# A SwiGLU block on one core: the down stage's first sums, a page's low part, and the second pair's stores and rebuilding steps rearranged

## Chip, cores and metric

The kernel runs on one core of a Trainium2 chip. The metric is the time of one execution on the device in microseconds (us), as the median of several runs. The engines are called TensorE (PE; its weight loads are PEld), VectorE (DVE), ScalarE (ACT), GpSimd (POOL) and SyncE (SP, which issues loads).

## What is computed

One transformer layer and a last norm, on x of 1024 tokens by 1024 channels, fp32. The change works in the last product pair of the layer, the SwiGLU:

```
mixed = jnp.concatenate([attn, pool], axis=-1)
x = x + jnp.einsum('bse,ed->bsd', mixed, w_out[layer])
h2 = rmsnorm(x, norm2_g[layer])
gate = jnp.einsum('bsd,df->bsf', h2, w_gate[layer])
up = jnp.einsum('bsd,df->bsf', h2, w_up[layer])
x = x + jnp.einsum('bsf,fd->bsd', jax.nn.silu(gate) * up, w_down[layer])
return rmsnorm(x, final_g)
```

D_FF is 2816. Ahead of it stand forgetting attention, a pooling mixer and the output projection, which the change does not touch.

## The kernel before

**Split products.** Each fp32 operand is split into a high part, which ACT copies out (line 120), and a low part, which DVE forms as operand minus high (line 121). A product is then three matmuls (`mm3`): high by high (L161), L162 and L163, each with one of the two low parts. A split operand is called a page; names end in `_h` and `_l`. A DVE instruction for a page of 128x1024 reads two operands from SBUF.

**Gate and up.** The 2816 columns are worked off in 11 pairs j = 0 to 10 of 2 x 128 columns. A pair is a Strassen scheme of seven products P1 to P7 between blocks of the turned activations (b11, b21, b22, t1 to t4) and a page of weights or of weight sums (`gu_page`; names `gu{j}_P1` and so on). POOL forms the weight sums s1 to s4 of the next pair from the raw loads r0 and r1 (L1091). From pair 2 on P3, and from pair 3 on P2 too, is itself done as seven quarter products Q1 to Q7 (banks `fineA`, `fineB`, `fineC`), each followed by an addition on DVE (L1289) from PSUM into an SBUF tile. A bank is used again by the next quarter, so TensorE waits for that addition. The pages of P3 come in two parts, a and b; their 128x256 sums (`fine_sums`, L1245) are on DVE but for part b of pair 10, which is on POOL. For b21 the quarter operands are rebuilt once, by a list of DVE steps (`fine_steps`, L1214, L1221; tiles `fine_b21..`, `fine2l_b21`, `b21l`) during pairs 1 and 2; the table `PACE` says how many steps are issued after each product.

**Order of work.** `todo` lists all (j, product). From pair 3 on the order is P1, P7, P2a, P6, P2b, P5, P3a, P4, P3b; in pairs 1 and 2 it is P1, P2, P6, P7, P5, P3a, P4, P3b. The page of an entry is issued two entries ahead (`next_page(*todo[i + 2])`), so page P1 of the next pair is issued at P4. A scheduler orders the instructions of each engine; `tc.issue_after(x)` keeps an instruction behind x. `mark` holds the last instruction of a kind: "page" (a low part), "hi" (a high part), "add" (a quarter's addition). The quarters Q5, Q6 and Q3 of P3 close a pair: their additions stand on DVE beside the low part of the next pair's P1.

**Features.** ACT, DVE and POOL turn the products into silu(gate) * up in the form that the down stage's own Strassen scheme wants: h11, h21, h22 (L1181, L1182) and f1 to f4 (L1190), which POOL forms. `spill` stores them to a scratch in DRAM (`hsdP1` to `hsdP7`, L1293), from ACT's queue, those of pair 10 from POOL's.

**Down stage.** The pairs are taken in four groups, (0, 1), (2, 3, 4), (5, 6, 7) and (8, 9, 10), each again with seven products in the order P1, P2, P6, P7, P5, P4, P3. Step i has a page of weights (tiles `d{i}_2` high, `d{i}_3` low) and one of features loaded back (`r_f{i}`; `d{i}_0` high, `d{i}_1` low), both made by `down_page(i)`. `down_sum` (L1379) forms the weight sums for P5, P6, P7 and P4 from the raw weights `r_wd0`, `r_wd1`; for the first group all four are on POOL, for the others on DVE. DVE adds the results to the residual (L1670). The first down page is made while pair 10 ends.

Of the kernel before, what the change touches and what calls it, by code (L numbers as in the profile page):

```python
# [30 lines left out]
NG = NF // 2  # L31
# [14 lines left out]
def tile_kernel(  # L46
# [952 lines left out]
    def gu_page(name, src, raw=None, cols=1024):  # L999
        n = count[0]  # L1000
        count[0] += 1
        hi, lo = page((("wh", "wl"), ("wh", "wl"), ("wr", "wr"))[n % 3], name)
        if cols < 1024:
            src = src.rearrange("p g e -> p (g e)")[:, 0:cols]
            mark["page"] = split(hi[:, 0:cols], lo[:, 0:cols], src)
            return hi, lo
        h2, l2 = (t.rearrange("p (g e) -> p g e", g=2) for t in (hi, lo))
        if raw:
            r = vpool.tile([P, 2, 1024], F32, tag=raw, bufs=1, name=f"r_{name}")[:, :, 0:512]
            for g in range(2):  # L1010
# [229 lines left out]
    def fine_sums(j, k, part, eng=nc.vector):  # L1240

        p0, p1, p2, p3 = (operands[j][k][:, n, h] for n in range(2) for h in QTR)
        later = ((p2, p3, p2, ALU.subtract), (p1, p1, p2, ALU.subtract), (p0, p0, p2, ALU.add))
        for out, in0, in1, op in ((p2, p0, p2, ALU.subtract),) if part == "a" else later:
            ins = eng.tensor_tensor(out=out, in0=in0, in1=in1, op=op)  # L1245
            mark["sum" if eng is nc.vector else "aside"] = ins
        summed.add((j, k, part))
# [50 lines left out]
    def after(j, k):  # L1298
# [12 lines left out]
        if k == "P2b":  # L1311
# [3 lines left out]
            nc.gpsimd.tensor_tensor(out=acc[1], in0=acc[1], in1=acc[0], op=ALU.mult)  # L1315
# [59 lines left out]
    def down_sum(b, k):  # L1375
        a0, a1 = dict(P5=("b12", "P1"), P6=("P3", "P5"), P7=("P3", "b12"), P4=("P2", "P6"))[k]
        t = blk_tile(SUMS[k], [P, len(GROUPS[b]), 512], F32, f"sum{k}_{b}")
        eng = nc.vector if b else nc.gpsimd
# [16 lines left out]
    def down_page(i):  # L1395
# [4 lines left out]
        lows = low, split(fh, fl, raw2.pop(i))  # L1400
# [20 lines left out]
    def next_page(j, k):  # L1421
        if (j, k) not in pages:
            if k[-1] in "ab":
                pages[j, k] = fine_page(j, k[:2], k[-1])
            else:
                pages[j, k] = gu_page(f"gu{j}_{k}", operands[j][k])
# [9 lines left out]
    PACE = {(1, "P1"): 1, (1, "P2"): 3, (1, "P6"): 3, (1, "P7"): 3, (2, "P1"): 2, (2, "P2"): 2, (2, "P6"): 1, (2, "P4"): 2, (2, "P3b"): 3}  # L1436
    waiting = []
    for i, (j, k) in enumerate(todo):
        shown = mark["page"]
        if i + 2 < len(todo) and (j < BOTH or k not in ("P1", "P2a")) and (j < BOTH - 1 or k != "P3a"):  # L1440
            with ExitStack() as order:
# [5 lines left out]
                if j >= BOTH and k in ("P7", "P6", "P2b", "P5"):  # L1447
                    if k == "P5":
                        fine_sums(j, "P3", "b", nc.vector if j < NG - 1 else nc.gpsimd)
# [4 lines left out]
                next_page(*todo[i + 2])  # L1454
# [6 lines left out]
        if j < BOTH:  # L1461
            while len(waiting) > 1:
                with tc.issue_after(mark["hi"].ins), tc.issue_after(mark["snap"].ins) if j == 2 else ExitStack():
# [42 lines left out]
        if j == NG - 1:  # L1506
# [20 lines left out]
        for _ in range(min(PACE.get((j, k), 2 if j < 2 else 0), len(finer))):  # L1527
            with tc.issue_after((shown if j == 2 and k != "P2" else mark["page"] if j else mark["h22", 0]).ins):
# [96 lines left out]
    for i, (b, k) in enumerate(steps2):  # L1625
# [3 lines left out]
        if b and k in ("P1", "P2", "P6") and (b, k) != (1, "P1"):  # L1629
# [85 lines left out]
```

## Time and profile before

| what | us |
|---|---|
| median of 3 runs | 1041.72 (1040.68 to 1042.95) |
| the profiled execution | 1040.65 |
| its span | 1038.9 |
| DVE busy | 776.1 (75%) |
| ACT busy | 471.6 (45%) |
| POOL busy | 405.5 (39%) |

The profile is that of one execution, and its instruction times are counted from the start of the span; 1.75 us of the execution lie outside it. In the timeline an engine's row gives start, duration, line, operation, and output <- input with partitions x elements. Numbers of tiles are left out there (`gu_P_l` is a low page of any pair); in the listings of the order below they stand, with a serial number behind. A bracket at the end of a row gives the idle time ahead of it and what released it. A DVE or POOL row starts when the instruction begins, also where it then stands still for another engine, so its duration can hold a wait. The rows of the windows give, for a stretch of time, each engine's busy time and count, the TensorE clock that was granted as a share of full speed, the share of time that the DMA engines were busy, and the GB/s.

### The profile page before, as it was taken

To read this page: it belongs to the slowest core of one execution; us is meant where nothing else is said; L and a number is where in the kernel's file an instruction comes from. 1 tells how busy PE (TensorE), PEld (TensorE's weight loads), DVE (VectorE), ACT (ScalarE), POOL (GpSimd) and SP (SyncE) were. 2 spreads that over 40 slices of the span, in tenths; PEclk is the share of its full clock that TensorE was granted. 3 is DMA by queue.
4 is the path that set the end of the run, shared out by engine and by line. 5 is a ranking of instruction groups with operands and counts; after the bars stand their busy time and mean duration, and the time that the engine had idled before them with its cause. 6 is when DMAs were issued, how large, how long until landed. Compare 5 with 4: busy or idle time off the path is not lost.

```text
span 1038.9 us, 15118 instructions
## 1 busy us (share of the span) xinstructions
PE 1022.6 (98%) x5428; PEld 878.7 (85%) x5428; DVE 776.1 (75%) x1219; ACT 471.6 (45%) x759; POOL 405.5 (39%) x322
## 2 busy tenths in 40 slices
PE   9999999999999999999999999999999899999997
PEld 8988888998888888888788888888888678888886
DVE  7465566776886488986977776876775899888887
ACT  7434355655665266442343443334334333333346
POOL 4350121213345042547547546555566900000045
PEclk9999999999999999999999999999999999999999
DMA  7214424233742142342223342332346764353424
GB/s 250 53 49 141 106 79 115 71 104 85 252 160 90 59 149 84 96 136 96 79 82 105 107 131 75 112 123 75 108 132 224 263 243 152 129 194 102 153 92 162
DMA packets 108795, 130.28 MB, mean 125 GB/s; under 512 B 8040, under 2 KB 71024, under 8 KB 108720
## 3 DMA queue, kind: packets, MB, share of 16 engines
q1 hardware_dynamic: 97216, 108.18, 33.3%
q10 hardware_dynamic: 10784, 19.16, 4.8%
q0 software_dynamic: 720, 1.97, 0.6%
q8 instruction: 43, 0.70, 0.3%
q14 instruction: 32, 0.26, 0.1%
HBM read 86.29 MB, written 33.03 MB: 115 GB/s over the span
## 4 chain that ended last, share of the span: by engine, by line
PE 95%; DVE 2%; issue 1%; DMA 1%; POOL 0%; ACT 0%; POOLq 0%; SPq 0%; DVEq 0%; ACTq 0%
PE gu_P L161 10%; PE gu_P L162 10%; PE gu_P L163 10%; PE d L162 6%; PE d L163 6%; PE d L161 6%; PE po L657 3%; PE tp L643 3%; PE o L161 3%; PE qk L162 3%; PE qk L163 3%; PE qk L161 3%; PE o L162 3%; PE o L163 3%; PE v L374 2%; PE z L618 2%
## 5 line engine op out<-in xcount | busy, mean ns | idle before, releaser
L162 PE MATMUL d<-d,d 128*128 128x512 f32 (+1 forms) x308 | 120.1, 391 | 4.7 <-DVE d L121 4.7
L163 PE MATMUL d<-d,d 128*128 128x512 f32 (+1 forms) x308 | 119.7, 390 | 0.0
L629 POOL TENSOR_SCALAR p<-p,rr 128x128 f32<-128x128 f32 (+3 forms) x64 | 48.5, 763 | 175.2 <-DVE rr L628 143.0
L161 PE MATMUL d<-d,d 128*128 128x512 f32 x308 | 108.3, 389 | 0.0
L120 ACT ACTIVATE d<-r_f 128x1536 fp32r<-128x1536 f32 (+1 forms) x28 | 38.8, 1384 | 119.0 <-PE d L162 114.3
L162 PEld LDWEIGHTS d<-d,d 128*128 128x128 f32 x308 | 58.3, 189 | 17.4 <-DVE d L121 5.3
L121 DVE TENSOR_TENSOR gu_P_l<-s,gu_P_h 128x1024 fp32r<-128x1024 f32 (+1 forms) x38 | 60.6, 1604 | 14.2 <-ACT gu_P_h L120 14.0
L1566 POOL TENSOR_SCALAR sse<-sse 128x1 f32<-128x1 f32 x7 | 3.5, 493 | 172.0 <-ACT junk L1562 172.0
L163 PEld LDWEIGHTS d<-d,d 128*128 128x128 f32 x308 | 58.3, 189 | 12.0
L161 PEld LDWEIGHTS d<-d,d 128*128 128x128 f32 x308 | 58.1, 189 | 12.0
L626 ACT ACTIVATE p<-p,mn 128x128 f32<-128x128 f32 (+3 forms) x64 | 49.3, 772 | 32.4 <-DVE mn L620 29.5
L121 DVE TENSOR_TENSOR gu_P_l<-r,gu_P_h 128x1024 fp32r<-128x1024 f32 x24 | 55.0, 2294 | 8.4 <-ACT gu_P_h L120 5.5
L121 DVE TENSOR_TENSOR d<-r_f,d 128x1536 fp32r<-128x1536 f32 (+1 forms) x28 | 54.7, 1954 | 7.0 <-ACT d L120 7.0
L648 DVE TENSOR_TENSOR tl<-tp,th 128x512 fp32r<-128x512 f32 (+1 forms) x80 | 49.4, 633 | 10.6 <-ACT th L647 9.6
L120 ACT ACTIVATE gu_P_h<-s 128x1024 fp32r<-128x1024 f32 (+1 forms) x38 | 36.4, 964 | 41.0 <-POOL f L1190 7.2
L1670 DVE TENSOR_TENSOR x2f_s<-d,x2f_s 128x512 f32<-128x512 f32 x64 | 42.6, 685 | 11.2 <-PE d L163 11.2
L163 PE MATMUL qk<-hTh,l_qk 128*128 128x512 f32 x128 | 50.7, 396 | 0.0
L161 PE MATMUL qk<-hTh,h_qk 128*128 128x512 f32 x128 | 50.6, 395 | 0.0
L162 PE MATMUL qk<-hTl,h_qk 128*128 128x512 f32 x128 | 50.4, 394 | 0.0
L647 ACT ACTIVATE th<-tp 128x512 fp32r<-128x512 f32 (+1 forms) x80 | 42.4, 550 | 14.9 <-PE tp L643 12.2
L1154 ACT ACTIVATE sn_sU<-gu_P 128x512 f32<-128x512 f32 x44 | 26.2, 595 | 45.6 <-PE gu_P L163 45.5
L620 DVE CUSTOM_DVE_ANT_0 p<-z,wmask 128x128 f32<-128x128 f32 (+3 forms) x64 | 33.7, 535 | 13.4 <-PE z L618 9.5
(1180 smaller groups left out, 3351.7 us busy)
## 6 DMA issues: line engine op xcount, KB each, us to landing
r_f<-hsdP SPq DMA_DIRECT2D x77, 256.0 KB
r<-in_w_gate_dram SPq DMA_DIRECT2D x44, 256.0 KB
r<-in_w_up_dram SPq DMA_DIRECT2D x44, 256.0 KB
r_wd<-in_w_down_dram SPq DMA_DIRECT2D x22, 512.0 KB
hsdP<-f ACTq DMA_DIRECT2D x40, 256.0 KB
s<-hi SPq DMA_DIRECT2D x64, 128.0 KB
hsdP<-h ACTq DMA_DIRECT2D x23, 256.0 KB
x<-in_x_dram SPq DMA_DIRECT2D x8, 512.0 KB
```

The lines of the kernel that those rows point to most:

```text
L120: mark["hi"] = nc.scalar.activation(out=hi, in_=src, func=AF.Copy)
L121: return eng.tensor_tensor(out=lo, in0=src, in1=f32(hi), op=ALU.subtract)
L161: nc.tensor.matmul(ps, lh, rh, start=start, stop=False, **kw)
L162: nc.tensor.matmul(ps, lh, rl, start=False, stop=False, **kw)
L163: mark["mm"] = nc.tensor.matmul(ps, ll, rh, start=False, stop=stop, **kw)
L620: nc.vector.tensor_tensor_reduce(out=pr[:, n0:n1], in0=z, in1=wmask[:, S - n + n0 : S - n + n1], scale=1.0, scalar=mn, op0=ALU.add, op1=AL ...
L626: nc.scalar.activation(out=pr[:, :n], in_=pr[:, :n], func=AF.Exp, scale=-1.0, bias=mn, accum_out=rs)
L629: nc.gpsimd.tensor_scalar(out=pr[:, :n], in0=pr[:, :n], scalar1=rr, scalar2=1.0, op0=ALU.mult, op1=ALU.mult)
L643: nc.tensor.transpose(tp[:, w : w + P], probs[h, 2 * sb + a][:, s * P : (s + 1) * P], ident)
L647: nc.scalar.activation(out=th[:, :w], in_=tp[:, :w], func=AF.Copy)
L648: nc.vector.tensor_tensor(out=tl[:, :w], in0=tp[:, :w], in1=f32(th[:, :w]), op=ALU.subtract)
L1670: added = nc.vector.tensor_tensor(out=row, in0=ps, in1=row, op=ALU.add)
```

## The change

Six parts:

1. `gu_page` takes `between`. For page P1 of pairs 3 to 10 the low part is made in two instructions of 128x512, and the second is kept behind the addition of the quarter issued last (the Q6 of P3).
2. The 128x256 sums for part b of P3 in pair 10 go from POOL to DVE.
3. The four weight sums of the first group are divided: P5 on DVE, behind page P5 of pair 10; P6 and P7 on POOL, behind the product h11 of pair 10; P4 on DVE, in the down stage at step P6.
4. `down_page(0)` is issued one entry later, at P4, and its feature low part d0_1 is kept behind a quarter's addition.
5. `PACE`: rebuilding steps of b21 that were issued at P4 and P3b of pair 2 are issued at P6 and P7.
6. The stores of pair 1's features, and of P1 and P4 of pair 2, are no longer issued entry by entry in pair 2, but at P7, P3a, P4 and P3b by the rule of the later pairs.

```diff
@@ -996,7 +996,7 @@
 
-    def gu_page(name, src, raw=None, cols=1024):
+    def gu_page(name, src, raw=None, cols=1024, between=None):
         n = count[0]
@@ -1013,6 +1013,13 @@
                 mark["page"] = split(h2[:, g, :], l2[:, g, :], src[g])
+        elif between is not None:
+            mark["hi"] = nc.scalar.activation(out=h2, in_=src, func=AF.Copy)
+            for g in range(2):
+                with tc.issue_after(between.ins) if g else ExitStack():
+                    mark["page"] = nc.vector.tensor_tensor(
+                        out=l2[:, g, :], in0=src[:, g, :], in1=f32(h2[:, g, :]), op=ALU.subtract
+                    )
         else:
@@ -1237,13 +1244,12 @@
 
-    def fine_sums(j, k, part, eng=nc.vector):
+    def fine_sums(j, k, part):
 
...
         for out, in0, in1, op in ((p2, p0, p2, ALU.subtract),) if part == "a" else later:
-            ins = eng.tensor_tensor(out=out, in0=in0, in1=in1, op=op)
-            mark["sum" if eng is nc.vector else "aside"] = ins
+            mark["sum"] = nc.vector.tensor_tensor(out=out, in0=in0, in1=in1, op=op)
         summed.add((j, k, part))
@@ -1312,7 +1318,7 @@
                 nc.scalar.activation(out=acc[0], in_=acc[0], func=AF.Silu)
-            nc.gpsimd.tensor_tensor(out=acc[1], in0=acc[1], in1=acc[0], op=ALU.mult)
+            mark["h11"] = nc.gpsimd.tensor_tensor(out=acc[1], in0=acc[1], in1=acc[0], op=ALU.mult)
             feats["h11"] = acc[1]
@@ -1372,10 +1378,9 @@
 
-    def down_sum(b, k):
+    def down_sum(b, k, eng=nc.vector):
         a0, a1 = dict(P5=("b12", "P1"), P6=("P3", "P5"), P7=("P3", "b12"), P4=("P2", "P6"))[k]
         t = blk_tile(SUMS[k], [P, len(GROUPS[b]), 512], F32, f"sum{k}_{b}")
-        eng = nc.vector if b else nc.gpsimd
         eng.tensor_tensor(out=t, in0=moving[b, a0], in1=moving[b, a1], op=ALU.subtract)
@@ -1392,12 +1397,13 @@
 
-    def down_page(i):
+    def down_page(i, between=None):
         b, k = steps2[i]
...
         low = split(wh, wl, moving[b, k])
-        lows = low, split(fh, fl, raw2.pop(i))
+        with tc.issue_after(between.ins) if between else ExitStack():
+            lows = low, split(fh, fl, raw2.pop(i))
         stationary[i] = fh, fl, wh, wl
@@ -1418,12 +1424,12 @@
 
-    def next_page(j, k):
+    def next_page(j, k, between=None):
         if (j, k) not in pages:
...
             else:
-                pages[j, k] = gu_page(f"gu{j}_{k}", operands[j][k])
+                pages[j, k] = gu_page(f"gu{j}_{k}", operands[j][k], between=between)
         if j + 1 < NG:
@@ -1433,7 +1439,7 @@
 
-    PACE = {(1, "P1"): 1, (1, "P2"): 3, (1, "P6"): 3, (1, "P7"): 3, (2, "P1"): 2, (2, "P2"): 2, (2, "P6"): 1, (2, "P4"): 2, (2, "P3b"): 3}
+    PACE = {(1, "P1"): 1, (1, "P2"): 3, (1, "P6"): 3, (1, "P7"): 3, (2, "P1"): 2, (2, "P2"): 2, (2, "P6"): 3, (2, "P7"): 3}
     waiting = []
@@ -1446,21 +1452,21 @@
                     if k == "P5":
-                        fine_sums(j, "P3", "b", nc.vector if j < NG - 1 else nc.gpsimd)
+                        fine_sums(j, "P3", "b")
                     for name in ("page", "hi") + (("sum",) if k in ("P2b", "P5", "P7") else ()):
...
                     order.enter_context(tc.issue_after(mark["snap"].ins))
-                next_page(*todo[i + 2])
+                next_page(*todo[i + 2], mark["add"] if j >= BOTH - 1 and k == "P4" else None)
             if j >= BOTH and k == "P7":
...
         spills.clear()
-        if j < BOTH:
+        if j < BOTH - 1:
             while len(waiting) > 1:
-                with tc.issue_after(mark["hi"].ins), tc.issue_after(mark["snap"].ins) if j == 2 else ExitStack():
+                with tc.issue_after(mark["hi"].ins):
                     spill(waiting.pop(0))
@@ -1510,13 +1516,17 @@
                     down_load(par)
+                with tc.issue_after(mark["page"].ins):
+                    down_sum(0, "P5", nc.vector)
             if k == "P5":
-                with tc.issue_after(mark["aside"].ins):
-                    for key in ("P5", "P6", "P7", "P4"):
-                        down_sum(0, key)
+                with tc.issue_after(mark["h11"].ins):
+                    for key in ("P6", "P7"):
+                        down_sum(0, key, nc.gpsimd)
             if k == "P3a":
-                with tc.issue_after(mark["add"].ins), tc.issue_after(mark["hi"].ins):
-                    down_page(0)
+                mark["quarter"] = mark["add"]
+            if k == "P4":
+                with tc.issue_after(mark["quarter"].ins), tc.issue_after(mark["hi"].ins):
+                    down_page(0, mark["add"])
         if (j, k) == (0, "P4"):
@@ -1525,7 +1535,7 @@
         for _ in range(min(PACE.get((j, k), 2 if j < 2 else 0), len(finer))):
-            with tc.issue_after((shown if j == 2 and k != "P2" else mark["page"] if j else mark["h22", 0]).ins):
+            with tc.issue_after((shown if (j, k) == (2, "P1") else mark["page"] if j else mark["h22", 0]).ins):
                 finer.pop(0)()
@@ -1626,7 +1636,7 @@
         more = b + 1 < len(GROUPS)
-        if b and k in ("P1", "P2", "P6") and (b, k) != (1, "P1"):
+        if b and k in ("P1", "P2", "P6") and (b, k) != (1, "P1") or (b, k) == (0, "P6"):
             with tc.issue_after(added.ins):
```

What this does to the order. DVE at the end of pair 2, before (the names: `fineA_2P3` is a quarter's bank of pair 2, `sn2_sU41` the tile that it is added to, `gu3_P1` and `gu3_P7` pages of pair 3, `fine_b21..` tiles of the rebuilding):

```order
L1221 TENSOR_TENSOR fine_b2111_5628<-fine_b2111_5628,fine_b2100_5546 128x512
L1289 TENSOR_TENSOR sn2_sU41_5740<-fineB_2P3_5764,sn2_sU41_5740 128x256
L121 TENSOR_TENSOR gu3_P1_l_5811<-r0_3_5670,gu3_P1_h_5810 128x1024
L121 TENSOR_TENSOR fine2l_b21_5840<-fine_b2111_5628,fine2h_b21_5839 128x512
L1289 TENSOR_TENSOR sn2_sU41_5740<-fineA_2P3_5748,sn2_sU41_5740 128x256
L1178 TENSOR_TENSOR sn2_sU20_5659<-gu2_P70_5676,sn2_sU20_5659 128x512
L1181 TENSOR_TENSOR h21_2_5834<-gu2_P71_5689,sn2_sU21_5661 128x512
L1214 TENSOR_TENSOR fine_b2110_5871<-b21h_4435,b21l_4436 128x512
L1289 TENSOR_TENSOR sn2_sU41_5740<-fineA_2P3_5748,sn2_sU41_5740 128x256
L121 TENSOR_TENSOR gu3_P7_l_5844<-s3_3_5778,gu3_P7_h_5843 128x1024
```

and in the changed kernel (its line numbers are a few higher; L1020 is the half low part):

```order
L121 TENSOR_TENSOR gu2_P3b_l_5779<-s4_2_5436,gu2_P3b_h_5778 128x768
L1295 TENSOR_TENSOR sn2_sU41_5744<-fineB_2P3_5770,sn2_sU41_5744 128x256
L1020 TENSOR_TENSOR gu3_P1_l_5817<-r0_3_5670,gu3_P1_h_5816 128x512
L1295 TENSOR_TENSOR sn2_sU41_5744<-fineA_2P3_5754,sn2_sU41_5744 128x256
L1020 TENSOR_TENSOR gu3_P1_l_5817<-r0_3_5670,gu3_P1_h_5816 128x512
L1185 TENSOR_TENSOR sn2_sU20_5654<-gu2_P70_5675,sn2_sU20_5654 128x512
L1188 TENSOR_TENSOR h21_2_5842<-gu2_P71_5688,sn2_sU21_5656 128x512
L1295 TENSOR_TENSOR sn2_sU41_5744<-fineA_2P3_5754,sn2_sU41_5744 128x256
L121 TENSOR_TENSOR gu3_P7_l_5847<-s3_3_5784,gu3_P7_h_5846 128x1024
```

The rebuilding steps are gone from between the additions, and the low part of `gu3_P1` stands in two halves around the first of them. The steps stand earlier now, ahead of page P4 of pair 2:

```order
L1228 TENSOR_TENSOR fine_b2111_5623<-fine_b2111_5623,fine_b2100_5546 128x512
L121 TENSOR_TENSOR gu2_P3a_l_5667<-s4_2_5436,gu2_P3a_h_5666 128x1024
L1221 TENSOR_TENSOR fine_b2110_5701<-b21h_4435,b21l_4436 128x512
L121 TENSOR_TENSOR fine41_b21_5545<-fine_b2101_5548,fine40_b21_5544 128x512
L1252 TENSOR_TENSOR s4_2_5436<-s4_2_5436 128x256
L1228 TENSOR_TENSOR fine_b2110_5701<-fine_b2110_5701,fine_b2111_5623 128x512
L121 TENSOR_TENSOR fine2l_b21_5662<-fine_b2111_5623,fine2h_b21_5661 128x512
L1252 TENSOR_TENSOR s4_2_5436<-s4_2_5436 128x256 x2
L121 TENSOR_TENSOR b21l_4436<-fine_b2110_5701,b21h_4435 128x2x256
L121 TENSOR_TENSOR gu2_P4_l_5710<-r1_2_5387,gu2_P4_h_5709 128x1024
```

DVE from the end of pair 10 into the down stage, before (`d0_3` and `d0_1` are the low parts of the first down page, `x2f` the residual):

```order
L1289 TENSOR_TENSOR sn10_sU41_8402<-fineB_10P3_8436,sn10_sU41_8402 128x256
L121 TENSOR_TENSOR d0_3_8477<-r_wd0_0_8223,d0_2_8476 128x1024
L121 TENSOR_TENSOR d0_1_8475<-r_f0_8350,d0_0_8474 128x1024
L1289 TENSOR_TENSOR sn10_sU41_8402<-fineA_10P3_8420,sn10_sU41_8402 128x256
L1181 TENSOR_TENSOR h21_10_8503<-gu10_P71_8255,sn10_sU21_8348 128x512
L1289 TENSOR_TENSOR sn10_sU40_8400<-fineA_10P3_8420,sn10_sU40_8400 128x256
L121 TENSOR_TENSOR d1_3_8522<-r_wd1_0_8226,d1_2_8521 128x1024
L121 TENSOR_TENSOR d1_1_8520<-r_f1_8353,d1_0_8519 128x1024
L1670 TENSOR_TENSOR x2f_r1_8537<-d0_0_8565,x2f_r1_8537 128x512
L1341 TENSOR_TENSOR sn10_sU41_8402<-sn10_sU41_8402,sn10_sU40_8400 128x512
```

and in the changed kernel:

```order
L1295 TENSOR_TENSOR sn10_sU41_8412<-fineB_10P3_8442,sn10_sU41_8412 128x256
L121 TENSOR_TENSOR d0_3_8509<-r_wd0_0_8231,d0_2_8508 128x1024
L1295 TENSOR_TENSOR sn10_sU41_8412<-fineA_10P3_8426,sn10_sU41_8412 128x256
L121 TENSOR_TENSOR d0_1_8507<-r_f0_8358,d0_0_8506 128x1024
L1188 TENSOR_TENSOR h21_10_8501<-gu10_P71_8263,sn10_sU21_8356 128x512
L1295 TENSOR_TENSOR sn10_sU40_8410<-fineA_10P3_8426,sn10_sU40_8410 128x256
L121 TENSOR_TENSOR d1_3_8528<-r_wd1_0_8234,d1_2_8527 128x1024
L121 TENSOR_TENSOR d1_1_8526<-r_f1_8361,d1_0_8525 128x1024
L1347 TENSOR_TENSOR sn10_sU41_8412<-sn10_sU41_8412,sn10_sU40_8410 128x512
L1680 TENSOR_TENSOR x2f_r1_8543<-d0_0_8571,x2f_r1_8543 128x512
```

An addition now stands between `d0_3` and `d0_1`, and the product of the two `sn10_sU4` tiles is ahead of the residual's additions. On TensorE the first down step begins, in the changed kernel, with eight matmuls of L161 and L162, which need no `d0_1`; before, the third matmul was one of L163, which does.

POOL over the same stretch, before (`sumP5_0` is the first group's sum for P5, and so on):

```order
L1245 TENSOR_TENSOR s4_10_8109<-s4_10_8109 128x256 x3
L1379 TENSOR_TENSOR sumP5_0_8410<-r_wd0_0_8223 128x1024
L1379 TENSOR_TENSOR sumP7_0_8414<-r_wd1_0_8226,r_wd0_0_8223 128x1024
L1315 TENSOR_TENSOR sn10_sP11_8221<-sn10_sP11_8221,sn10_sP10_8219 128x512
L1182 TENSOR_TENSOR h22_10_8404<-h22_10_8404,qh22_10_8405 128x512
L1379 TENSOR_TENSOR sumP6_0_8412<-r_wd1_0_8226,sumP5_0_8410 128x1024
L1293 DMA hsdP1_10_4831<-sn10_sP11_8221 128x512
L1293 DMA hsdP4_10_4897<-h22_10_8404 128x512
L1379 TENSOR_TENSOR sumP4_0_8416<-r_wd1_0_8226,sumP6_0_8412 128x1024
```

and in the changed kernel:

```order
L1321 TENSOR_TENSOR sn10_sP11_8229<-sn10_sP11_8229,sn10_sP10_8227 128x512
L1384 TENSOR_TENSOR sumP6_0_8420<-r_wd1_0_8234,sumP5_0_8364 128x1024
L1384 TENSOR_TENSOR sumP7_0_8422<-r_wd1_0_8234,r_wd0_0_8231 128x1024
L1299 DMA hsdP1_10_4831<-sn10_sP11_8229 128x512
L1189 TENSOR_TENSOR h22_10_8414<-h22_10_8414,qh22_10_8415 128x512
L1299 DMA hsdP4_10_4897<-h22_10_8414 128x512
L1189 TENSOR_TENSOR h21_10_8501<-h21_10_8501,sn10_sU20_8354 128x512
L1299 DMA hsdP2_10_4842<-h21_10_8501 128x512
```

Two of the four sums and the 128x256 sums have left POOL, and the others stand ahead of h22.

## Prediction

> **What bounds the kernel now.** I read the page first: busy time, share of the span, instructions.
>
> ```profile
> PE 1022.6 (98%) x5428; PEld 878.7 (85%) x5428; DVE 776.1 (75%) x1219; ACT 471.6 (45%) x759; POOL 405.5 (39%) x322
> ```
>
> TensorE is busy for 98% of the span. The change alters no matmul, so it can only gain where TensorE stands still. Next I read TensorE's waits. The columns are total us, times and longest.
>
> ```profile
> PE d L162 <- DVE d L121: 4.7, 1, 4.7
> PE fineA_2P L161 <- DVE sn_sU L1289: 1.8, 2, 1.5
> PE fineA_10P L161 <- DVE sn_sU L1289: 1.0, 1, 1.0
> ```
>
> These three, 7.5 us, are waits for DVE, and all lie where the change works. They cost more than 7.5. After the 4.7 us wait the windows show this (PE busy, PEld, DVE, ACT, POOL, granted clock, DMA share, GB/s):
>
> ```profile
> 826.00:832.40 6.40, 1.73 (x8) 1.11 (x6) 6.40 (x3) 2.00 (x2) 5.69 (x7) 0.99 0.38 145
> 832.40:836.00 3.60, 3.56 (x9) 2.84 (x10) 3.60 (x6) 0.00 (x0) 0.00 (x0) 0.54 0.71 253
> ```
>
> For 3.6 us the granted clock is 0.54, so about (1 − 0.54) × 3.6 = 1.65 us are lost on top. Whether the shorter waits have such a tail, I read at their places below.
>
> Then the timeline around each wait, for the reason. In the down stage (start, us, engine, what):
>
> ```profile
> 817.82 4.89 DVE L121 TENSOR_TENSOR d<-r_f,d 128x1024 fp32r<-128x1024 f32 x1
> 825.63 5.62 DVE L121 TENSOR_TENSOR d<-r_f,d 128x1024 fp32r<-128x1024 f32 x1
> 831.18 1.21 DVE L121 TENSOR_TENSOR d<-sumP,d 128x1024 fp32r<-128x1024 f32 x1
> ...
> 817.42 0.54 POOL L1293 DMA_DIRECT2D hsdP<-h  x1
> 817.98 2.40 POOL L1379 TENSOR_TENSOR sumP<-r_wd,sumP 128x1024 f32<-128x1024 f32 x1
> 820.33 1.29 POOL L1182 TENSOR_TENSOR h<-h,sn_sU 128x512 f32<-128x512 f32 x1
> ...
> 825.83 1.30 POOL L1190 TENSOR_TENSOR f<-f,sn_sP 128x512 f32<-128x512 f32 x1
> 828.89 1.27 POOL L1190 TENSOR_TENSOR f<-h,f 128x512 f32<-128x512 f32 x1
> ...
> 826.66 1.07 PE L161 MATMUL d<-d,d 128*128 128x512 f32 x4
> 832.45 0.79 PE L162 MATMUL d<-d,d 128*128 128x512 f32 x1 [4.71 <-DVE d L121]
> ```
>
> A DVE subtraction of 128x1024 with two SBUF inputs takes 1.21 us when alone. The two of 4.89 and 5.62 us end 1.09 us after a POOL instruction ends (820.33 + 1.29, 828.89 + 1.27): they ran only when POOL had let go, and POOL ran at its own speed meanwhile. So DVE and POOL exclude each other on such operations. The Trainium skill has this as a rule (SBUF — State Buffer, section "SBUF: two separate sides"): a DVE operation with two SBUF inputs and a GpSimd operation hold a shared port pair as an exclusive lock, whichever starts first, for its whole instruction. By that rule the first would have run between 820.38 and 821.5, after one POOL operation; the trace differs, since POOL took two in a row.
>
> **The change part by part.** All times are those of the profiled execution: span 1038.9, 1040.65 us in all.
>
> *Second pair: rebuilding steps and stores.*
>
> ```profile
> 489.35 0.69 DVE L1214 TENSOR_TENSOR fine_b<-b21h,b21l 128x512 f32<-128x512 f32 x1
> 493.98 1.23 DVE L121 TENSOR_TENSOR gu_P_l<-s,gu_P_h 128x1024 fp32r<-128x1024 f32 x1 [3.94 <-ACT gu_P_h L120]
> 508.49 2.86 DVE L121 TENSOR_TENSOR fine2l_b<-fine_b,fine2h_b 128x512 fp32r<-128x512 f32 x1
> 511.28 0.41 DVE L1289 TENSOR_TENSOR sn_sU<-fineA_2P,sn_sU 128x256 f32<-128x256 f32 x1
> 512.81 2.60 DVE L1214 TENSOR_TENSOR fine_b<-b21h,b21l 128x512 f32<-128x512 f32 x1
> ...
> 509.85 0.39 PE L163 MATMUL gu_P<-t4h,gu_P_l 128*128 128x512 f32 x1
> 511.74 0.38 PE L161 MATMUL fineA_2P<-fine_b,gu_P3b_h 128*128 128x256 f32 x1 [1.51 <-DVE sn_sU L1289]
> 515.79 0.39 PE L161 MATMUL fineA_2P<-b22h,gu_P3b_h 128*128 128x256 f32 x1 [0.31 <-DVE sn_sU L1289]
> ```
>
> The additions that TensorE waits for stand behind two rebuilding steps of 2.86 and 2.60 us. The steps move to before page P4, into the stretch with the 3.94 us hole; five or six operations of about 0.69 there are 3.5 to 4.1 us. That hole is ACT's: its page copy stood behind stores in ACT's queue, which now come later. Without the steps the first addition ends by 508.9, since DVE is through with page P1 at 508.49; it is needed at 509.85 + 0.23 = 510.1. The other needs, at worst, one POOL sum (2.40), half a page (0.6), two PSUM operations (0.6 each) and itself: 513.5, and TensorE would come there at about 513.6. Both waits go. Start to start the first is 511.74 − 509.85 − 0.23 = 1.66; with the second and a refill after each (below, 0.1) 2.3 in all. Take **−2.3**. If the hole does not close, the steps run into page P4 and 1 us comes back. The later stores have no reader before the down stage.
>
> *Halves of the low part, pairs 3 to 10.* A typical place, pair 6:
>
> ```profile
> 658.96 3.22 DVE L121 TENSOR_TENSOR gu_P_l<-r,gu_P_h 128x1024 fp32r<-128x1024 f32 x1 [0.59 <-DMA r<-in_w_gate_dram]
> 662.10 0.41 DVE L1289 TENSOR_TENSOR sn_sU<-fineA_6P,sn_sU 128x256 f32<-128x256 f32 x1
> 663.63 0.41 DVE L1289 TENSOR_TENSOR sn_sU<-fineA_6P,sn_sU 128x256 f32<-128x256 f32 x1
> ...
> 658.69 2.40 POOL L1091 TENSOR_TENSOR s<-r,r 128x1024 f32<-128x1024 f32 x1 [1.78 <-DMA r<-in_w_up_dram]
> 661.15 3.29 POOL L1091 TENSOR_TENSOR s<-r 128x1024 f32<-128x1024 f32 x1
> ...
> 662.58 0.36 PE L161 MATMUL fineA_6P<-fine_b,gu_P3b_h 128*128 128x256 f32 x1
> 666.11 0.28 PE L161 MATMUL fineA_6P<-b22h,gu_P3b_h 128*128 128x256 f32 x1
> ```
>
> The low part waits for POOL's first sum (661.09), then runs, and the addition at 662.10 just suffices. Halved, the first half ends at 661.6, the addition at 662.0. But POOL's second sum now gets in between the halves (661.6 to 664.0); the second half ends at 664.6, two PSUM operations of 0.6 follow, and the Q5 addition ends at 666.1 instead of 664.04, just when TensorE wants it (666.11). So a hidden loss of 0.1 to 0.25 us in five pairs (0.76 in all, start to start) is traded for up to 0.2 at Q3, and the next page's low part may lose its turn to POOL's fourth sum and come some 0.35 late in six pairs. Bounds −0.8 and +2.1; neither end has a nearer row, so the middle, **+0.7**.
>
> *First group's sums.* They take POOL 2.40 each and DVE 1.21. sumP5 goes to DVE behind page P5:
>
> ```profile
> 793.42 1.75 DVE L121 TENSOR_TENSOR gu_P_l<-s,gu_P_h 128x1024 fp32r<-128x1024 f32 x1 [0.61 <-ACT gu_P_h L120]
> 795.10 0.41 DVE L1289 TENSOR_TENSOR sn_sP<-fineA_10P,sn_sP 128x256 f32<-128x256 f32 x1
> 794.05 2.27 POOL L1182 TENSOR_TENSOR h<-h,sn_sU 128x512 f32<-128x512 f32 x1
> 797.04 0.28 PE L161 MATMUL fineA_10P<-fine_b,gu_P2b_h 128*128 128x256 f32 x1
> ```
>
> POOL holds until 796.32, sumP5 then ends at 797.4 and the addition at 797.75 instead of 795.5. TensorE, which passes at 797.04 without waiting, now waits 0.76, and 0.1 to refill: **+0.9** (0 if sumP5 comes first, 2 if sumP7 also holds up page P3b, which follows).
>
> *P3's last sums* go from POOL to DVE, 1.2 us among DVE's idle stretches near 800: nothing. If those were filled, page P4 would come 1.2 us late.
>
> *First down page later, low part split.*
>
> ```profile
> 812.24 2.31 DVE L121 TENSOR_TENSOR d<-r_f,d 128x1024 fp32r<-128x1024 f32 x1
> 814.47 0.41 DVE L1289 TENSOR_TENSOR sn_sU<-fineA_10P,sn_sU 128x256 f32<-128x256 f32 x1
> 813.55 0.40 PE L163 MATMUL gu_P<-t4h,gu_P_l 128*128 128x512 f32 x1
> 814.94 0.39 PE L161 MATMUL fineA_10P<-b22h,gu_P3b_h 128*128 128x256 f32 x1 [0.99 <-DVE sn_sU L1289]
> 815.16 0.28 PE L162 MATMUL fineA_10P<-b22l,gu_P3b_h 128*128 128x256 f32 x1
> ```
>
> The addition no longer stands behind the 2.31 us: it comes near 813.5, needed by 813.8. 814.94 − 813.55 − 0.23 = 1.16; the next starts 0.22 later where 0.12 is usual, a refill of 0.1 and no slow clock: **−1.3** (−0.6 if POOL's store holds up d0_3 too). d0_1 then ends near 814.9; the stage starts near 815.4, and with eight matmuls (0.23 each) put ahead that do not need it, TensorE wants it about 817.2.
>
> *Sums off POOL in the down stage.* sumP6 and sumP4 leave the stretch 813 to 820, so d0_1, h21, an addition, d1_3 and d1_1 follow one another on DVE and d1_1 ends near 819 instead of 822.71. POOL's features, which need the sum behind it, start about 819.7, four us earlier. d2_1 then waits for one, two or all of the features: d2_3 (1.21) ends at 824.4, 825.7 or 827.6. TensorE wants it near 827.4. The wait, 4.87 start to start, goes, and with it the slow clock: **−6.5**. What comes next is sumP4, now on DVE (1.2), with about 2 us to spare before the fourth page.
>
> Sum: −2.3 + 0.7 + 0.9 − 1.3 − 6.5 = −8.5, so 1040.65 − 8.5 = 1032.15 for a profiled execution. The median of the runs stood 1.07 above that execution (1041.72): **1033.1 us**.
>
> **The rivals.**
>
> *The lock eats the down gain.* The features still exclude DVE for longer than they did, d2_3 comes after 830, TensorE waits 3 us or more and the clock falls. For it: two POOL instructions in a row went ahead of DVE at 817.82, and four at 825.63, each time as DVE came during a POOL store; the new order has such stores. Against it: POOL's queue ends four us earlier. Then −6.5 is near nothing: −2, 1039.7 us. The Trainium skill leans that way (Perfetto Trace Analysis, "Optimizing Scalar/DVE Operations"): moving work between GpSimd and DVE might not help, as they share a port. The rows of 4.89 and 5.62 agree about the port; that moving does not help, no run here shows yet.
>
> *Slower: the first half shut out.* If POOL's second sum follows its first without letting DVE in, the half runs at 663.5, its addition ends at 664.5 where TensorE, without its hidden loss, wants 662.3: 2.2 us in each pair with such an overlap, about six: +13.2 − 9.2 (the sum without the halves' 0.7) = +4, 1045.7 us. It decides from five pairs on (9.2 / 2.2). Against it: at 661.15 POOL's second sum took 3.29, so DVE did get in.
>
> *Not done:* rebuilding steps or stores that wait for something else and give the second pair's gain back, along with a shut-out at pair 10: no more than 3 us, 1036.
>
> **How the numbers follow.** The forecast, its waits at pair 10 included, 0.77; the third rival 0.06; the lock 0.10; slower 0.07. A measurement of this kernel tells about 0.2% (2.1 us) from no change. The lock's 1039.7 lies on that bound, so half of it and a little more counts as the same: faster 0.86, same 0.07, slower 0.07. The range: at best −0.8 for the halves and 0 for sumP5, −10.9, 1030.8; at worst +2.1, +2, −0.6 and 1 us left at d2, −4.3, 1037.4, and a little towards the lock's case: 1038.
>
> **What would show it.** TensorE's waits without `d`, `fineA_2P` Q6 and with about 0.8 at the second quarter page of pair 10; no stretch of clock near 0.5 at 826 to 836; d2_3 ended before 828; the addition between the halves by 662.0 less the earlier gain. A wait on `gu_P` pages in most pairs, or a granted clock near 0.5 in the down stage, would make it wrong.

## The result and the profile after

| | before | changed |
|---|---|---|
| median, us | 1041.56 (1040.68 to 1042.95) | 1032.93 (1032.53 to 1034.69) |
| the profiled execution, us | 1040.65 | 1034.69 |
| its span, us | 1038.9 | 1032.9 |

The ratio is 0.9919, with a 95% interval of 0.9902 to 0.9936: 6.7 to 10.2 us faster. The forecast was 1033.1. A second measurement of the changed kernel, on another occasion, gave 1033.73 and 0.9919 (0.9905 to 0.9933).

First the busy times of the changed kernel, then TensorE's waits (total us, times, longest):

```profile
PE 1021.6 (99%) x5428; PEld 877.9 (85%) x5428; DVE 771.9 (75%) x1232; ACT 472.0 (46%) x759; POOL 399.4 (39%) x317
```

```profile
PE fineA_10P L161 <- DVE sn_sP L1295: 0.9, 1, 0.9
PE o L161 <- ACT h_wo L120: 0.6, 1, 0.6
PE gu_P L161 <- DVE qh L1185: 0.5, 1, 0.5
...
PE fineA_10P L161 <- DVE sn_sU L1295: 0.2, 1, 0.2
```

The row of 4.7 us for `d` is gone, and so is the row with the two waits of pair 2; of the 1.0 us at the end of pair 10, 0.2 are left. Two new waits, of 0.9 and 0.5, stand where the change works. The one of `o` on `h_wo` lies in the output projection, which the change does not touch.

The windows of the down stage after the change (PE busy, PEld, DVE, ACT, POOL, granted clock, DMA share, GB/s) have no hole and no slow clock:

```profile
820.00:826.00 6.00, 6.00 (x28) 4.98 (x27) 6.00 (x8) 2.01 (x2) 4.35 (x3) 1.00 0.84 316
826.00:832.00 6.00, 6.00 (x28) 4.97 (x27) 6.00 (x7) 2.01 (x2) 4.26 (x6) 1.00 0.73 266
```

TensorE's order is the same in both kernels up to the down stage, so its lost time can be added up place by place: the time between the starts of two matmuls, less the usual 0.23 us (0.12 for the quarters' 256 columns). Every kernel of this study is in the table, in us. A slow clock that follows a wait is counted with it.

| kernel | P4 of pair 2 | additions of pair 2 | pairs 3 to 9 | pair 10, P2's quarter | end of pair 10 | down stage |
|---|---|---|---|---|---|---|
| before | 0 | 2.34 | 0.76 | 0 | 1.27 | 6.50 |
| changed | 1.14 | 0 | 0.66 | 1.21 | 0.51 | 0 |
| changed, second measurement | 1.19 | 0 | 0.81 | 0.45 | 0.51 | 0 |
| e1 all sums on GpSimd | 1.29 | 0 | 1.03 | 0 | 4.44 | 2.24 |
| e2 sums alone | 0 | 2.35 | 0.97 | 0.52 | 1.14 | 0 |
| e3 whole low part | 1.18 | 0 | 0.95 | 0.53 | 0.53 | 0 |
| e4 early stores | 2.00 | 0 | 1.03 | 0.45 | 0.68 | 0 |
| e5 before, stores on ACT | 0 | 2.34 | 0.71 | 0 | 1.26 | 1.57, later 2.3 |
| e6 changed, stores on ACT | 1.24 | 0 | 1.21 | 0.46 | 0 | 1.02 |
| e7 two steps later | 0.10 | 0 | 1.50 | 0.34 | 2.35 (P4, P3b) | 0.28 |
| e8 sumP5 behind additions | 1.34 | 0 | 0.90 | 0 | 0.50 | 0 |
| e9 four repairs | 0 | 0 | 2.75 | 0 | 0 | 0 |
| e10 three repairs | 1.29 | 0 | 1.01 | 0 | 0 | 0 |
| e12 first page early | 1.31 | 0 | 0.76 | 1.01 | 1.64 | 0 |

Before loses 10.87 us in these columns, the changed kernel 3.52: the change is worth 7.35. Its profiled execution shows 6.0 of span, since 1.15 us were lost at 270 us already, in the wait on `h_wo`. The run with the sums alone has the same wait and the second measurement only 0.4 of it, so it is a matter of the single execution.

Now the three places with something left, in the changed kernel. In pair 2 (start, us, engine, what):

```profile
493.50 3.48 DVE L1228 TENSOR_TENSOR fine_b<-fine_b,fine_b 128x512 f32<-128x512 f32 x2
496.90 2.31 DVE L121 TENSOR_TENSOR gu_P3a_l<-s,gu_P3a_h 128x1024 fp32r<-128x1024 f32 x1
503.15 1.21 DVE L121 TENSOR_TENSOR gu_P_l<-r,gu_P_h 128x1024 fp32r<-128x1024 f32 x1
...
492.46 2.27 POOL L1197 TENSOR_TENSOR f<-h,sn_sU 128x512 f32<-128x512 f32 x1
494.69 1.74 POOL L1197 TENSOR_TENSOR f<-h,f 128x512 f32<-128x512 f32 x1
...
505.02 0.50 PE L161 MATMUL gu_P<-t4h,gu_P_h 128*128 128x512 f32 x1 [0.47 <-DVE qh L1185]
```

The hole of 3.94 us is closed, but the steps moved there meet GpSimd's features of pair 1: two that take 0.69 each alone take 3.48 together. Page P4 is ready at 504.4, the reading of the bank behind it (`qh`) comes late, and TensorE waits.

At pair 10, where sumP5 stands now:

```profile
793.56 2.10 DVE L121 TENSOR_TENSOR gu_P_l<-s,gu_P_h 128x1024 fp32r<-128x1024 f32 x1 [0.61 <-ACT gu_P_h L120]
795.59 2.31 DVE L1384 TENSOR_TENSOR sumP<-r_wd 128x1024 f32<-128x1024 f32 x1
797.82 0.41 DVE L1295 TENSOR_TENSOR sn_sP<-fineA_10P,sn_sP 128x256 f32<-128x256 f32 x1
...
794.54 2.27 POOL L1189 TENSOR_TENSOR h<-h,sn_sU 128x512 f32<-128x512 f32 x1
...
798.28 0.39 PE L161 MATMUL fineA_10P<-fine_b,gu_P2b_h 128*128 128x256 f32 x1 [0.95 <-DVE sn_sP L1295]
```

And at its end, the first down page's low part against a store and h22 on GpSimd:

```profile
812.39 2.76 DVE L121 TENSOR_TENSOR d<-r_wd,d 128x1024 fp32r<-128x1024 f32 x1
815.07 0.41 DVE L1295 TENSOR_TENSOR sn_sU<-fineA_10P,sn_sU 128x256 f32<-128x256 f32 x1
...
812.06 0.66 POOL L1299 DMA_DIRECT2D hsdP<-sn_sP  x1
812.75 1.31 POOL L1189 TENSOR_TENSOR h<-h,qh 128x512 f32<-128x512 f32 x1
```

VectorE comes at 812.39, while GpSimd issues a store; h22 begins after it and runs its usual 1.3; VectorE ends 1.09 after that, at 815.15.

### The profile page after: what moved, and what is told of

It reads as the page before. It is cut to its first block, busy times and chain, and to the rows that moved or that the text cites. A ratio compares the mean times of both kernels' runs of the same rounds, so it can differ in the third digit from the quotient of the medians.

```text
span 1032.9 us, 15118 instructions
## 1 busy us (share of the span) xinstructions
PE 1021.6 (99%) x5428; PEld 877.9 (85%) x5428; DVE 771.9 (75%) x1232; ACT 472.0 (46%) x759; POOL 399.4 (39%) x317
## 3 DMA queue, kind: packets, MB, share of 16 engines
q0 software_dynamic: 720, 1.97, 0.5%
## 4 chain that ended last, share of the span: by engine, by line
PE 87%; DVE 4%; POOL 3%; issue 2%; DMA 2%; ACT 1%; ACTq 0%; SPq 0%; POOLq 0%; DVEq 0%
PE gu_P L161 8%; PE gu_P L162 8%; PE gu_P L163 8%; PE d L161 6%; PE d L162 6%; PE d L163 6%; PE po L657 3%; PE tp L643 3%; PE qk L161 3%; PE qk L162 3%; PE qk L163 3%; PE o L162 3%; PE o L163 3%; PE o L161 3%; PE v L374 2%
## 5 line engine op out<-in xcount | busy, mean ns | idle before, releaser
L162 PE MATMUL d<-d,d 128*128 128x512 f32 (+1 forms) x308 | 118.7, 388 | 0.0
L163 PE MATMUL d<-d,d 128*128 128x512 f32 (+1 forms) x308 | 118.0, 388 | 0.0
L161 PE MATMUL d<-d,d 128*128 128x512 f32 x308 | 108.0, 388 | 0.0
L162 PEld LDWEIGHTS d<-d,d 128*128 128x128 f32 x308 | 57.8, 188 | 12.1 <-DVE d L121 0.2
L161 PEld LDWEIGHTS d<-d,d 128*128 128x128 f32 x308 | 57.8, 188 | 11.9
L163 PEld LDWEIGHTS d<-d,d 128*128 128x128 f32 x308 | 57.8, 188 | 11.8
L121 DVE TENSOR_TENSOR gu_P_l<-s,gu_P_h 128x1024 fp32r<-128x1024 f32 (+1 forms) x38 | 48.2, 1278 | 12.4 <-ACT gu_P_h L120 12.2
L121 DVE TENSOR_TENSOR d<-r_f,d 128x1536 fp32r<-128x1536 f32 (+1 forms) x28 | 45.7, 1634 | 6.6 <-ACT d L120 6.5
L163 PE MATMUL qk<-hTh,l_qk 128*128 128x512 f32 x128 | 50.7, 396 | 0.0
L161 PE MATMUL qk<-hTh,h_qk 128*128 128x512 f32 x128 | 50.6, 395 | 0.0
L162 PE MATMUL qk<-hTl,h_qk 128*128 128x512 f32 x128 | 50.4, 394 | 0.0
L643 PE MATMUL tp<-ident,p 128*128 128x128 f32 x288 | 43.2, 274 | 0.0
```

The costliest lines, as they stand in the source:

```text
L121: return eng.tensor_tensor(out=lo, in0=src, in1=f32(hi), op=ALU.subtract)
L161: nc.tensor.matmul(ps, lh, rh, start=start, stop=False, **kw)
L162: nc.tensor.matmul(ps, lh, rl, start=False, stop=False, **kw)
L163: mark["mm"] = nc.tensor.matmul(ps, ll, rh, start=False, stop=stop, **kw)
L643: nc.tensor.transpose(tp[:, w : w + P], probs[h, 2 * sb + a][:, s * P : (s + 1) * P], ident)
```

## The experiments

**The two theories.** Mine: the down stage's 6.5 us come from the sums that left GpSimd's queue. The rival: they come from the later, divided first down page. Then come the costs: the halves, the stores, the lock. Where an experiment was a single execution, its time is not compared; its profile is, by the table.

**e1, all four sums on GpSimd.** From the changed kernel:

```diff
-                with tc.issue_after(mark["page"].ins):
-                    down_sum(0, "P5", nc.vector)
...
-                    for key in ("P6", "P7"):
+                    for key in ("P5", "P6", "P7", "P4"):
                         down_sum(0, key, nc.gpsimd)
...
-        if b and k in ("P1", "P2", "P6") and (b, k) != (1, "P1") or (b, k) == (0, "P6"):
+        if b and k in ("P1", "P2", "P6") and (b, k) != (1, "P1"):
```

> The changed kernel with all four first-group sums on GpSimd again (P5, P6, P7, P4 issued behind h11 of pair 10), everything else as changed. Theory: the gain of the down stage comes from the two sums that left GpSimd's queue. Then TensorE waits again for the low part d2_3, 4 to 5 us in one piece, the granted clock is near 0.5 for some 3.6 us behind it, and the wait of 1.0 us that sumP5 makes at the second quarter page of pair 10 is gone: 6.4 - 1.2 = 5 us more than the changed kernel, about 1038. Rival (the later, divided first down page is what freed the down stage): no wait in the down stage, 1.2 us less than the changed kernel, about 1031.7.

Measured: 1041.06 us, ratio to before 0.9989 (0.9980 to 0.9998). All but 1 us of the gain is gone, though the later, divided page is still there, so the rival falls. But I had the place wrong, and the size (1038). The timeline of e1:

```profile
811.93 5.09 DVE L121 TENSOR_TENSOR d<-r_wd,d 128x1024 fp32r<-128x1024 f32 x1
...
827.50 5.06 DVE L121 TENSOR_TENSOR d<-r_f,d 128x1024 fp32r<-128x1024 f32 x1
...
811.59 0.66 POOL L1299 DMA_DIRECT2D hsdP<-sn_sP  x1
812.28 1.30 POOL L1189 TENSOR_TENSOR h<-h,qh 128x512 f32<-128x512 f32 x1
813.53 2.39 POOL L1384 TENSOR_TENSOR sumP<-r_wd,sumP 128x1024 f32<-128x1024 f32 x1
...
827.11 1.30 POOL L1197 TENSOR_TENSOR f<-f,sn_sP 128x512 f32<-128x512 f32 x1
...
817.40 0.39 PE L161 MATMUL fineA_10P<-b22h,gu_P3b_h 128*128 128x256 f32 x1 [2.57 <-DVE sn_sU L1295]
833.75 0.50 PE L162 MATMUL d<-d,d 128*128 128x512 f32 x1 [1.97 <-DVE d L121]
```

Now d0_3 is shut out already, for 5.09 us, by h22 and one of the sums, and d2_1 for 5.06 by the features, which come later for it. TensorE waits 2.57 at the end of pair 10 and 1.97 at d2_3. With the slow clock behind the first (1.59) this is 6.7 us in two pieces, against before's 6.5 in one; 0.5 of it the changed kernel has at the end of pair 10 too.

**e2, the sums alone**, in the kernel before:

```diff
+            mark["h11"] = nc.gpsimd.tensor_tensor(out=acc[1], in0=acc[1], in1=acc[0], op=ALU.mult)
...
+                with tc.issue_after(mark["page"].ins):
+                    down_sum(0, "P5", nc.vector)
...
+                with tc.issue_after(mark["h11"].ins):
+                    for key in ("P6", "P7"):
+                        down_sum(0, key, nc.gpsimd)
...
+        if b and k in ("P1", "P2", "P6") and (b, k) != (1, "P1") or (b, k) == (0, "P6"):
```

> The kernel before with the division of the first group's sums alone (P5 on VectorE behind page P5, P6 and P7 on GpSimd behind h11, P4 on VectorE in the down stage). Theory: the 4.7 us wait and the slow clock behind it go (-6.4), sumP5 makes its wait of 1 us at pair 10 (+1.2), the waits of pair 2 and the 1.0 us at the end of pair 10 stay: about 1036.4. Rival (the later first down page did it): 4.7 us stay, 1042.5 or more.

Measured: 1035.9 us, ratio 0.9941 (0.9924 to 0.9957). TensorE's waits of e2 begin with pair 2; `d` has no row. The windows (columns as above) show no slow clock:

```profile
PE fineA_2P L161 <- DVE sn_sU L1289: 1.8, 2, 1.5
```

```profile
824.00:830.00 6.00, 6.00 (x28) 4.96 (x27) 5.80 (x6) 2.62 (x4) 5.90 (x6) 1.00 0.76 277
830.00:834.00 4.00, 4.00 (x19) 3.30 (x18) 4.00 (x5) 1.00 (x2) 1.49 (x3) 1.00 0.50 199
```

So the sums alone give the whole of the down stage's 6.5 us, less 0.5 for sumP5. Both directions agree: this part is shown.

**e12, the first down page as before**, in the changed kernel:

```diff
-                mark["quarter"] = mark["add"]
-            if k == "P4":
-                with tc.issue_after(mark["quarter"].ins), tc.issue_after(mark["hi"].ins):
-                    down_page(0, mark["add"])
+                with tc.issue_after(mark["add"].ins), tc.issue_after(mark["hi"].ins):
+                    down_page(0)
```

> The changed kernel with its first down page as before: issued one entry earlier, the two low parts next to each other on VectorE. Theory (the sums freed the down stage, the page only its own place): TensorE's wait at the end of pair 10 grows from 0.5 us to 1.3 or more, since the addition stands behind d0_1 again; the down stage still has no wait at d2_3. Rival (the page's place is needed too): a wait of over 1 us at d2_3, and a slow clock if it is over 2.5.

Measured: 1.64 us at the end of pair 10 instead of 0.51, and no wait in the down stage. The page's place is worth 1.1 us, all of it at pair 10.

**e3, the low part whole**, in the changed kernel:

```diff
-                next_page(*todo[i + 2], mark["add"] if j >= BOTH - 1 and k == "P4" else None)
+                next_page(*todo[i + 2])
```

> The changed kernel with the low part of page P1 in one instruction again. By the prediction's term (+0.7 for the halves) this gains 0.7 us; by the two traces (0.76 us hidden before, 0.66 us after in pairs 3 to 9) it changes 0.1 us: the small waits ahead of Q3 go, those ahead of Q5 in pairs 3 and 5 to 8 come back. Rival (the halves do the work they look made for): waits of 0.3 us or more ahead of Q5 in most pairs, 1.5 us or more in all.

Measured: 0.95 us in pairs 3 to 9, against 0.66 and 0.81 in the two profiles with halves; the waits stand ahead of Q5 again instead of Q3. Since the kernels with halves, whose code for these pairs is the same, lie between 0.66 and 1.21 (e9 and e7 apart), the halves have no effect that can be told.

**e4, the stores as before**, in the changed kernel:

```diff
-        if j < BOTH - 1:
+        if j < BOTH:
             while len(waiting) > 1:
-                with tc.issue_after(mark["hi"].ins):
+                with tc.issue_after(mark["hi"].ins), tc.issue_after(mark["snap"].ins) if j == 2 else ExitStack():
```

> The changed kernel with pair 1's and pair 2's stores issued entry by entry again (part 6 undone), the rebuilding steps where the change put them. Theory: the page copy of P5 stands behind the stores in ScalarE's queue again, VectorE has its 3.9 us hole near 490, the steps run 2 to 3 us later and page P4 of pair 2 is late by 2 to 4 us instead of 0.6. Rival (the stores cost nothing, the steps alone set page P4's time): TensorE's wait at P4 stays at 0.5 to 0.7 us.

Measured: 2.00 us at P4 instead of 1.14. The direction is the theory's, the size is not: the stores' later place is worth 0.9 us, not 2 to 3.

**e5 and e6, pair 10's stores from ACT's queue**, e5 in the kernel before, e6 in the changed one. GpSimd's two instructions in a row, which went ahead of VectorE, had a store close by; this takes the stores out of its queue.

```diff
-    spill(sum(waiting, []) + spills, nc.gpsimd)
+    spill(sum(waiting, []) + spills)
```

> The kernel before with the stores of pair 10's features issued from ScalarE's queue instead of GpSimd's; the sums stay as before. Theory (a store in GpSimd's queue is what makes VectorE lose its turn over several GpSimd instructions): d1_1 takes 2.5 us or less instead of 4.89 and d2_1 3 or less instead of 5.62, the wait of 4.7 us shrinks below 2.5 and the slow clock is gone, 4 us faster in the down stage. Rival (GpSimd keeps the port over any instructions that stand ready in its queue, stores or not): both stay above 4.5 us and the wait stays above 4.

> The changed kernel with the same move of the stores. Theory of the store: d0_3, which came during a store and took 2.76, takes 1.3, and the rest of the wait at the end of pair 10 (0.41 and 0.1 refill) goes: 0.5 us less. Rival: d0_3 stands still as long as before, behind h22 alone, and the 0.5 stays. Either way ScalarE's page copies may stand behind stores that wait for features; if they do, TensorE waits at the third down page.

The timeline of e5, to be held against the rows of 4.89 and 5.62 us:

```profile
818.20 3.41 DVE L121 TENSOR_TENSOR d<-r_f,d 128x1024 fp32r<-128x1024 f32 x1
825.02 2.11 DVE L121 TENSOR_TENSOR d<-r_f,d 128x1024 fp32r<-128x1024 f32 x1
...
813.81 6.71 POOL L1379 TENSOR_TENSOR sumP<-r_wd,sumP 128x1024 f32<-128x1024 f32 x2
820.48 2.27 POOL L1182 TENSOR_TENSOR h<-h,sn_sU 128x512 f32<-128x512 f32 x1
824.76 1.29 POOL L1190 TENSOR_TENSOR f<-f,sn_sP 128x512 f32<-128x512 f32 x1
826.01 2.27 POOL L1190 TENSOR_TENSOR f<-sn_sP,sn_sU 128x512 f32<-128x512 f32 x1
...
829.42 0.50 PE L162 MATMUL d<-d,d 128*128 128x512 f32 x1 [1.30 <-DVE d L121]
```

The same instructions now take turns: d1_1 gets in at 820.5, after one sum, and h takes 2.27 because it waits for d1_1; d2_1 gets in after one feature. d1_1's 3.41 missed the 2.5 that I gave it, because its one sum itself began late, behind d1_3. The wait falls from 4.71 to 1.30 and the slow clock is gone, with all four sums still on GpSimd. In e6 the 0.51 at the end of pair 10 is gone, but d0_3 takes 2.06 and not the 1.3 that I gave it: h22, with no store ahead of it, had begun at 811.34, 0.31 us before d0_3 came, and d0_3 still waited for it. Both pay elsewhere: in e6 ACT's page copies stand behind stores that wait for features (1.02 at d3); the 2.3 at later down steps in e5 were not followed up.

**e7, two rebuilding steps later**, and **e8, sumP5 behind the additions**, in the changed kernel:

```diff
-    PACE = {..., (2, "P6"): 3, (2, "P7"): 3}
+    PACE = {..., (2, "P6"): 3, (2, "P7"): 1, (3, "P1"): 2}
```

> The changed kernel with the last two rebuilding steps (a subtraction and the low part of b21) issued at P1 of pair 3 instead of P7 of pair 2. Theory: page P4 of pair 2 is late by 0.6 us because VectorE has these steps, lengthened by GpSimd's features, ahead of it: without two of them (0.6 each) the 1.1 us at P4 and the quarter behind it go, and no wait comes at pair 3. Rival: the steps before them are what makes P4 late, or ScalarE's copy is: the wait stays above 0.4 us.

```diff
-                with tc.issue_after(mark["page"].ins):
+                with tc.issue_after(mark["add"].ins):
                     down_sum(0, "P5", nc.vector)
```

> The changed kernel with sumP5 on VectorE behind the next quarter's additions of pair 10 instead of ahead of them. Theory: the wait there (1.1 us and 0.1 refill in the changed kernel's profile) goes, and page P3a is not late, since VectorE is idle for 1.2 us there. Rival: sumP5 makes another wait at P3a or delays sumP6 and with it d2_3: as much comes back.

e7: P4 of pair 2 is on time (0.10), but 0.63 comes at pair 3's P2, so half is given back. It also lost 2.35 at P4 and P3b of pair 10, where the edit changes nothing: there VectorE stood behind two GpSimd operations, its 128x256 sums behind the product h11 (802.69 to 804.02) and page P4 behind sumP6,

```profile
804.23 3.42 DVE L121 TENSOR_TENSOR gu_P_l<-r,gu_P_h 128x1024 fp32r<-128x1024 f32 x1
803.98 2.58 POOL L1384 TENSOR_TENSOR sumP<-r_wd,sumP 128x1024 f32<-128x1024 f32 x1
```

because sumP6 began 0.25 us before page P4 instead of after it (in the changed kernel 805.63 against 804.44). e8: the wait at pair 10 is gone, page P3a is not late and nothing comes back.

**e9 and e10, the repairs together, and the changed kernel again.** e9 takes e8's edit, puts e7's two steps at `(2, "P3b")`, and adds

```diff
-                with tc.issue_after(mark["h11"].ins):
+                with tc.issue_after(mark["h11"].ins), tc.issue_after(mark["page"].ins):
                     for key in ("P6", "P7"):
...
-    spill(sum(waiting, []) + spills, nc.gpsimd)
+    for first in (True, False):
+        due = [e for e in sum(waiting, []) + spills if (e[0] in ("P1", "P4")) == first]
+        spill(due, nc.scalar if first else nc.gpsimd)
```

e10 is e9 without the move of the steps.

> The changed kernel with four repairs: the last two rebuilding steps behind page P7 of pair 3, sumP5 behind the quarter's additions of pair 10, sumP6 and sumP7 on GpSimd behind page P4 of pair 10, and the stores of h11 and h22 of pair 10 from ScalarE's queue. Theory: the waits that the change left or made go: 1.1 us at P4 of pair 2, 1.2 at the second quarter page of pair 10, 0.5 at its end; 2.8 us less than the changed kernel, about 1030.2, with no wait of over 0.3 us between pair 2 and the end. Rival: they only move on, as in the runs with one repair each: between 1031.5 and 1033.

> The repaired kernel with the rebuilding steps where the change put them. Theory: 1.1 us at P4 of pair 2 comes back and nothing else, so it lies between the two runs beside it. Rival: the waits of pair 10 come back as well or instead, since they are a matter of which engine comes first.

> The changed kernel itself once more, on the same chip as its repaired form. It should show the same waits: 1.1 us at P4 of pair 2, 0.4 to 1.2 at the second quarter page of pair 10, 0.5 at its end, none in the down stage; about 1033.

Measured: e9 1032.96 us, ratio 0.9912 (0.9898 to 0.9927); the changed kernel on the same occasion 1033.73, 0.9919 (0.9905 to 0.9933). The intervals lie on each other: e9 is not shown to be faster, and the 1030.2 that I gave it did not come. The table says why: pair 10 is clean in e9 and in e10, but the moved steps make 1.9 us of waits at P2 of pair 3. e10 loses 2.30 us in all, against 3.52 and 2.96 in the changed kernel's profiles; its one execution took 1032.52, and whether it beats the changed kernel was not settled.

## Why the prediction was right

Term by term, against the changed kernel's first profile:

| term | predicted | measured |
|---|---|---|
| sums off GpSimd in the down stage | −6.5 | −6.50 |
| rebuilding steps and stores, pair 2 | −2.3 | −1.20 |
| first down page | −1.3 | −0.76 |
| sumP5 on VectorE | +0.9 | +1.21 |
| halves | +0.7 | −0.10 |
| sum | −8.5 | −7.35 |

- **The down stage** was right in size and in cause: the wait of 4.87 and the slow clock behind it, which the waits alone do not show, went, and e1 and e2 tie both to the sums. TensorE wanted d2_3 near 828.2 and had it in time, with no stretch of clock near 0.5. d2_3 ended at 827.56, and that it lies at the last of my three times (827.6) is chance: only two features went ahead, as in the middle one (825.7), one holding up d2_1 and one d2_3, but they started at 821.57 where I had 819.7. VectorE was later because d0_3 and d1_3 were each held up too (2.76 and 2.27 instead of 1.21), so d1_1 ended at 820.87 and not near 819.
- **Pair 2** was mis-sized. The additions' waits went, as worked out. The step that failed is "five or six operations of about 0.69 there are 3.5 to 4.1 us": beside GpSimd's features two of them took 3.48. I had named the price ("the steps run into page P4 and 1 us comes back"), but for a hole that does not close. The hole closed and 1.14 came back all the same: I took the uncontended row for a place where GpSimd was at work.
- **The first page** came out at the lower end that I had given for "POOL's store holds up d0_3 too", and it was the store: e6 takes it away, h22 comes earlier, and the rest of the wait goes.
- **sumP5** cost what was said, within what it varies: 0.34 to 1.21 in the kernels that have it there. It hangs on whether a feature of pair 9 or page P5 gets the port first (GpSimd 793.29 against 793.56 in the changed kernel).
- **The halves**: I took the middle between −0.8 and +2.1 and nothing happened. The mechanism was seen rightly: in pair 6 the first addition ends at 662.36 and the Q5 one at 666.35, where I had 662.0 and 666.1, and the execution as a whole is 0.4 us later there (the Q3 matmul at 666.52 instead of 666.11). But a page never lost its turn to the fourth sum, which I had charged with the most; in five pairs the page was ahead by only 0.1 us (in pair 6, 667.07 against 667.17).

That 1033.1 met the measured 1032.93 so closely is luck. The sum was 1.15 us too hopeful, and I added 1.07 us because the median of before stood that far above its profiled execution; the median of the changed kernel stands 1.8 below its own. Before's profiled execution was also one of its better ones: its granted clock was 0.998, while 17 of the 23 executions of before in the experiments had 0.995 or 0.996, and all of the changed kernel 0.998 or 0.999. Most executions of before thus had more slow clock than the table counts, at places that no trace shows.

The lock rival had its mechanism right and its place wrong: GpSimd went ahead at d0_3 (2.76), not at d2_3. The sentence of the Trainium skill that stood beside it (Perfetto Trace Analysis, "Optimizing Scalar/DVE Operations") says that moving work between the two engines might not help; here it helped, for e2 is that move alone, 0.9941.

## What to carry to other kernels

A wait of TensorE should be priced with the granted clock behind it: 4.7 us cost 6.5. When an operation moves into a hole, look whether GpSimd works in that stretch, and take its duration from a row beside such work, not from a free one. An edit that orders only one engine leaves it to chance which of two engines comes first, so a repair can be eaten by a race elsewhere, and the place-by-place sum shows it where the total does not.

## What the runs showed of the hardware that was not expected

- **Where VectorE came during a store of GpSimd's, it lost its turn.** GpSimd's following operations went ahead of it one after another (4.89, 5.62 and 5.09 us for an operation of 1.21); with the stores moved the two took turns (3.41 and 2.11, e5). The profiles of all runs, counted from the gate and up stage on, agree: nine low parts came during a store with GpSimd operations behind it, and each time one to three of these went first; 512 were held up for over 0.3 us by a GpSimd operation that was already running, and 511 of them got in right behind it. The one exception is e1's d2_1: it came at 827.50, while a feature ran and no store, and two more features went ahead (5.06). Why a store does this is not settled, nor how long it lasts: in e1 d0_3 got in at 815.92, with sumP4 still to come, where a store was next in GpSimd's queue.
- **A shorter wait was followed by a slow clock too.** In e1 2.57 us of waiting were followed, from 1.1 us after the restart, by a slow clock (PE busy, PEld, DVE, ACT, POOL, granted clock, DMA share, GB/s):

```profile
819.00:822.00 3.00, 3.00 (x9) 2.41 (x8) 3.00 (x4) 1.11 (x2) 1.17 (x2) 0.54 1.02 317
822.00:826.00 4.00, 4.00 (x20) 3.29 (x19) 4.00 (x5) 0.70 (x1) 1.10 (x2) 1.00 0.64 202
```

  After the 1.97 us in the same execution there was none. The Trainium skill (TensorE: Matmul & The Clock Gate, section "What's actually happening") puts the fall to half rate after an idle window of about 3.4 us; the 4.71 us agree, the 2.57 do not.
